# A two-layer transformer trunk on one core: elementwise sums and products of two SBUF tiles all on VectorE, and new prices in the order planner

## The chip, the cores and the metric

The kernel runs on one core of a Trainium2 chip. The metric is the device time of one execution in microseconds. Before the change the median of 3 runs is 1422.42 us (1422.35 to 1424.1).

In the profile the engines are PE (TensorE matmul), PEld (TensorE weight load), DVE (VectorE), ACT (ScalarE), POOL (GpSimd) and SP (SyncE, which issues the DMAs here).

## The reference

The reference is a trunk of two layers on 512 tokens of width 1024, all in float32. Each layer is three residual blocks with a norm before and after:

```
for layer in range(2):
    y = mixer(rms_norm(x, g[0]));            x = x + rms_norm(y, g[1])
    y = memory_cross_attention(rms_norm(x, g[2]), rms_norm(mem, mem_norm_g), ...)
    x = x + rms_norm(y, g[3])
    y = swiglu(rms_norm(x, g[4]), wg, wu, wd);   x = x + rms_norm(y, g[5])
```

The mixer of layer 0 joins 8 heads of forgetting attention (softmax with a cumulated log gate) with 8 heads of sparse attention (compressed, selected and window branches with gates, partial rotary embedding on q and k). The mixer of layer 1 is differential attention of 8 heads (two softmaxes, p = a1 - lam * a2) with a norm on each head. The cross attention has 4 heads over 256 memory tokens. The SwiGLU has width 2816: `(silu(h @ wg) * (h @ wu)) @ wd`.

## The kernel before

Every float32 operand of a large product is split in two float32r parts, hi and lo = x - hi, and a product is three matmuls: hi*hi, hi*lo, lo*hi (`mm`). So each tile of weights or activations needs one copy to hi (ScalarE) and one subtraction to lo (VectorE, `split`, line 556). Weights come in tiles of 128x1024 ("raw"), 3 buffers, and go to pairs of "w", "pt" or "u" tiles.

Tokens stand in four blocks of 128. The stages in order of time: norm and projections of layer 0, forgetting attention, sparse attention, then `last_heads` (line 965), in which each token block goes through `chain` (line 849): output projection, `post_norm` (line 643), cross attention, a second `post_norm`, and the norm before the SwiGLU. Then `ffn` (line 999) with 22 columns blocks of 128 in groups of three (`up` makes one), ending in `post_norm` again. Layer 1 repeats this with the differential attention. `post_norm` takes a row of 1024 in two halves. Where the product stands in PSUM, it multiplies it with the factor and the gain into a tile "q" and adds that to x; where it stands in SBUF, it multiplies by the gain and then adds. For the first half (i = 0) this sum or product of two SBUF tiles is on GpSimd, for the second on VectorE. The factor comes from `rstd` (line 611): squares with a row sum on ScalarE, a sum on VectorE, and a power on GpSimd (the rows `c<-c,mhalf`). In `up`, the lo part of the activation is a subtraction on GpSimd, 22 to a layer.

The order of the instructions on all queues isn't that of the source. `note` (line 135) records every operation with its dependences and a price in ns (`price`, line 182); `order` (line 215) plans up to 14 rounds forward (`forward`, line 284) and backward (`backward`, line 239) in a list schedule over the five engines, keeps the round with the shortest planned span, and `issue` (line 487) emits it; so all profile rows have line 491. TensorE operations also have a `load`: the planned least time from the start of the one before to its own. `lend` (line 398) lets GpSimd take a waiting VectorE sum, difference or product of SBUF tiles where VectorE's planned backlog is long enough; the emitted engine is then GpSimd. The planner knows nothing of an engine slowing another.

Of the kernel before, what the change touches and what calls it, by code (L numbers as in the profile page):

```python
# [11 lines left out]
F32 = mybir.dt.float32  # L12
F32R = mybir.dt.float32r
# [4 lines left out]
PSUM = bass.MemoryType.PSUM  # L18
# [7 lines left out]
DH = 64  # L26
# [7 lines left out]
LAM_INIT = 0.8 - 0.6 * math.exp(-0.3 * 1)  # L34
LEAD = 2
KA = 6
ROWS = slice(0, DH), slice(DH, P)
ORDER = 0, 4, 5, 6, 7, 1, 8, 9, 10, 11, 12, 13, 2, 3
FILL0, FILL1, STAGE, LATE = 0.0, 1.2, 2.0, 30
# [48 lines left out]
class Plan:  # L88
# [9 lines left out]
    NEAR, FEW = 10000.0, 12  # L98
    AHEAD, EARLY, RING = 50000.0, 60000.0, 8
    ALPHA, BETA = 1.0, 2.0  # L100
    FLEX, MORE, HOLD = 100.0, 1.5, 5000.0

    def __init__(self, nc):
        self.nc = nc
# [30 lines left out]
    def note(self, eng, method, args, kw):  # L135
        aps = [("out" if i == 0 else "in", v) for i, v in enumerate(args) if isinstance(v, bass.AP)]
        if "out" in kw or "out_" in kw:
            aps = [("in", v) for _, v in aps]
        aps += [("out" if k in ("out", "accum_out") else "in", v) for k, v in kw.items() if isinstance(v, bass.AP)]

        op = dict(eng=eng.name, call=(eng, method, args, kw), cost=0.0, deps=set(), tiles=set(), prio=len(self.ops))
        i = len(self.ops)
        for kind, ap in aps:
            if ap.space == bass.MemoryType.DRAM and not str(ap.tensor.name).startswith("xsave"):
                continue
            name, p0, p1, mask = self.region(ap)
            if name in self.tags:
                op["tiles"].add(name)
            acc = self.seen.setdefault(name, ([], []))
            for w in (0,) if kind == "in" else (0, 1):  # L150
                for j, q0, q1, m in acc[w]:
                    if q0 < p1 and p0 < q1 and m & mask:
                        op["deps"].add(j)
            if ap.space == PSUM and kind == "in":

                op["deps"].update(j for j, *_ in acc[1] if self.ops[j]["eng"] != eng.name)
            acc[0 if kind == "out" else 1].append((i, p0, p1, mask))
        op["deps"].discard(i)
        op["group"] = i
        op["dma"] = method == "dma_start"  # L160
        if method == "matmul" and not kw["start"]:
            op["group"] = self.last_group[args[0].tensor.name]
        if method == "matmul":
            self.last_group[args[0].tensor.name] = op["group"]
        op["cost"] = self.price(eng.name, method, args, kw, [v for _, v in aps])

        op["alt"] = {}
        if eng.name == "vector" and method in ("tensor_sub", "tensor_add", "tensor_mul") and op["cost"] > self.FLEX \
                and all(ap.space != PSUM for _, ap in aps):
            op["alt"]["gpsimd"] = self.price("gpsimd", method, args, kw, [v for _, v in aps])  # L170
        op["load"] = 53.0 if method != "matmul" else self.free(args[1]) / (1.2 if args[1].dtype == F32R else 2.4)
        self.ops.append(op)
        return op

# [7 lines left out]
    def price(self, eng, method, args, kw, aps):  # L182
        n = max([self.free(a) for a in aps] + [1])
        if method == "dma_start":
            size = 1
            for _, k in aps[0].ap:
                size *= k
            return size * 4 / 360.0
        if eng == "tensor":
            if method == "transpose":  # L190
                return 107.0
            c = self.free(args[2]) / 2.4
            return max(25.0, 2.5 + (c if args[2].dtype == F32R else 4 * c))
        if eng == "scalar":
            extra = sum(isinstance(kw.get(k), bass.AP) for k in ("bias", "scale", "accum_out"))
            return (52 if aps[1].space == PSUM else 95) + 0.83 * n + 93 * extra
        if eng == "vector":
            psum = any(a.space == bass.MemoryType.PSUM for a in aps)
            n = n + 62 * sum(isinstance(v, bass.AP) and self.free(v) == 1 for v in args[2:3])
            if method == "reciprocal":  # L200
                return 60 + 8 * n
            if method in ("tensor_copy", "tensor_scalar", "memset") and not psum:
                return 65 + 0.52 * n
            return 65 + 1.04 * n
        if eng == "gpsimd":
            if method == "tensor_tensor":
                return 260 + 200 * n
            if method in ("tensor_sub", "tensor_add", "tensor_mul"):
                return 100 + 2.3 * n
            if method == "memset":  # L210
                return 30 + 0.84 * n
            return (322 if len(aps) > 3 else 222) + 0.84 * n
        raise ValueError(method)

    def order(self):
        ops = self.ops
        n = len(ops)
        self.eng0 = [o["eng"] for o in ops]
        self.succ = [[] for _ in range(n)]
        for i, o in enumerate(ops):  # L220
            for j in o["deps"]:
                self.succ[j].append(i)
        best = None
        prio = [float(o["prio"]) for o in ops]
        for _ in range(self.ROUNDS):
            for i, o in enumerate(ops):
                prio[o["group"]] = min(prio[o["group"]], prio[i])
            prio = [prio[o["group"]] for o in ops]
            for k, o in enumerate(self.firsts):
                prio[o["group"]] = k - 1e9  # L230
            r = self.forward(prio, self.AHEAD - best[0] if best else math.inf)
            if best is None or r[0] < best[0]:
                best = r
            prio = self.backward(r)
        self.span, self.at, self.fin, out = best[:4]
        self.eng = best[5]
        return out

    def backward(self, run):

        span, at, fin, out, reuse, eng = run
        ops, n = self.ops, len(self.ops)
        pred = [list(o["deps"]) for o in ops]
        for j, i in reuse:
            pred[i].append(j)
# [5 lines left out]
        ready = {e: [] for e in engines}  # L251
# [6 lines left out]
        while ev:  # L258
            now = ev[0][0]
# [4 lines left out]
            for e in engines:  # L264
                h = ready[e]
                while h and busy[e] <= now + 1e-9:
                    i = heapq.heappop(h)[1]
                    cost = ops[i]["cost"] if eng[i] == self.eng0[i] else ops[i]["alt"][eng[i]]
                    end = now + cost
                    if ops[i]["dma"]:  # L270
                        end += 2000
# [11 lines left out]

    def forward(self, prio, far):

        ops, eng, succ = self.ops, list(self.eng0), self.succ
        n = len(ops)
        left = [len(o["deps"]) for o in ops]
        users, queue = {}, {}
# [105 lines left out]
                    heapq.heappush(heap, (top, i))  # L395
            return found

        def lend(e, f):

            wait = busy[e] - now  # L400
            for top, i in sorted(ready[e]):
                c = ops[i]["alt"].get(f)
                if c and wait > self.MORE * (c - ops[i]["cost"]) \
                        and not any(at[j] < now + c and prio[j] < top + self.HOLD for j in soon[f]):
                    ready[e].remove((top, i))
                    heapq.heapify(ready[e])
                    eng[i] = f
                    heapq.heappush(ready[f], (top, i))
                    return
                wait += ops[i]["cost"]  # L410

        while done < n:
            if not events:
                raise RuntimeError(f"no order found; stuck on {sorted(stuck)} at instruction {min(set(range(n)) - set(out))} of {n}")
# [18 lines left out]
            again = True  # L433
            while again:
                again = False
                if busy["gpsimd"] <= now + 1e-9 and not ready["gpsimd"] and busy["vector"] > now:
                    lend("vector", "gpsimd")
                for e, heap in ready.items():
                    while heap and busy[e] <= now + 1e-9:
                        if e in ("vector", "scalar", "gpsimd"):  # L440
# [8 lines left out]
                        o = ops[i]  # L449
                        out.append(i)  # L450
                        done += 1
                        cost = o["cost"] if e == self.eng0[i] else o["alt"][e]
                        if o["dma"]:
                            at[i] = now
                            busy[e] = now + 60
# [22 lines left out]
                        for j in succ[i]:  # L478
                            left[j] -= 1
                            at[j] = max(at[j], fin + self.LAT.get(e[0] + eng[j][0], 100.0))  # L480
                            if not left[j]:
                                heapq.heappush(events, (at[j], seq, "op", j))
                                soon[eng[j]].add(j)
                                seq += 1
        return max(ends), at, ends, out, reuse, eng

    def issue(self, tc):
        with tc.manual_schedule():
# [5 lines left out]
class Trunk:  # L494
# [148 lines left out]
    def post_norm(self, ys, g, x, tb):  # L643

        nc = self.nc
        r = self.rstd(ys)
        c0 = 0
        for i, y in enumerate(ys):
            s = slice(c0, c0 + y.shape[-1])
            c0 = s.stop  # L650
            if ys[i].space == PSUM:
                h = self.qtile()
                nc.vector.scalar_tensor_tensor(h, ys[i], r, g[:, s], op0=ALU.mult, op1=ALU.mult)
                (nc.vector if i else nc.gpsimd).tensor_add(x[tb][:, s], x[tb][:, s], h)
            else:
                (nc.vector if i else nc.gpsimd).tensor_mul(ys[i], ys[i], g[:, s])
                nc.vector.scalar_tensor_tensor(x[tb][:, s], ys[i], r, x[tb][:, s], op0=ALU.mult, op1=ALU.add)

    def xtile(self):
# [339 lines left out]
    def ffn(self, l, x, hT):  # L999
# [5 lines left out]
        def up(c):  # L1005
# [11 lines left out]
            nc.vector.scalar_tensor_tensor(b, th, 0.5, pu, op0=ALU.mult, op1=ALU.mult)  # L1017
            at = acts[c] = self.unit()
            nc.scalar.activation(at[:, 0:512], b, AF.Copy)
            nc.gpsimd.tensor_sub(at[:, 512:1024], b, at[:, 0:512].bitcast(F32))  # L1020

        where = self.pt_tiles
        yacc = None
# [622 lines left out]
```

## Time and profile before

| | us |
|---|---|
| median of 3 runs | 1422.42 |
| the profiled execution, its own time | 1422.67 |
| span of its trace, first to last instruction | 1421.0 |
| mean granted TensorE clock, share of full | 0.996 |

The span is what the rows below divide; 1.67 us of the profiled execution's own time lie outside it. Busy time of an engine is the time in which at least one of its instructions runs; matmuls are pipelined, so a busy TensorE may still be short of its peak rate. A row "x6" of a timeline is six like instructions in one stretch. Times in timelines are from the start of the span.

### The profile page before, as it was taken

The numbers are of one execution on the slowest core, as the hardware profiler recorded it, in microseconds if no ns is written. First come the engines' busy times: TensorE is split into PE (matmuls) and PEld (weight loads), VectorE is DVE, ScalarE is ACT, GpSimd is POOL, SyncE is SP. The second block draws the span as 40 slices with busy tenths as digits, with TensorE's granted clock in tenths as the row PEclk, the third lists the DMA queues.
The fourth block names the chain that finished last, engine by engine and source line by source line (L and its number), as shares of the span: only waits on it lengthen the run. The fifth ranks groups of instructions, "written<-read, shape, count | busy, mean of one in ns | idle before, by whom it ended". The sixth has DMA issues, their size and how long they took to land.

```text
span 1421.0 us, 21566 instructions
## 1 busy us (share of the span) xinstructions
PE 1383.2 (97%) x8003; PEld 1204.0 (85%) x8003; DVE 833.7 (59%) x1851; ACT 725.0 (51%) x1606; POOL 355.9 (25%) x429
## 2 busy tenths in 40 slices
PE   7999999999899999999999999999989999999997
PEld 6788988889788888888889999988878888888886
DVE  5667899498842333433466888876984233343344
ACT  5768879488643122223245677786863322222322
POOL 2203334244320121012031233312552012101202
PEclk9999999999999999999999999999999999999999
DMA  7251112321233233324321321243234323332411
GB/s 218 65 150 47 46 45 87 107 74 61 89 119 89 89 104 90 114 78 134 105 74 54 95 91 61 77 147 104 85 92 121 89 84 110 89 108 85 119 60 60
DMA packets 150425, 132.05 MB, mean 93 GB/s; under 512 B 6928, under 2 KB 134096, under 8 KB 150320
## 3 DMA queue, kind: packets, MB, share of 16 engines
q1 hardware_dynamic: 150320, 130.67, 30.2%
q8 instruction: 63, 1.03, 0.3%
q14 instruction: 42, 0.34, 0.1%
HBM read 126.26 MB, written 4.19 MB: 92 GB/s over the span
## 4 chain that ended last, share of the span: by engine, by line
PE 84%; DVE 7%; ACT 3%; DMA 2%; POOL 2%; issue 2%; SPq 0%; POOLq 0%; DVEq 0%; ACTq 0%
PE ps L491 84%; DVE q L491 2%; DVE x L491 1%; DVE u L491 1%; ACT q L491 1%; DVE c L491 1%; DMA raw<-in_ev_w_in_dram 1%; POOL c L491 1%; POOL q L491 1%; ACT u L491 1%; DVE pt L491 1%; DMA pt<-in_ev_w_in_dram 0%; DVE w L491 0%; ACT pt L491 0%; POOL x L491 0%
## 5 line engine op out<-in xcount | busy, mean ns | idle before, releaser
L491 PE MATMUL ps<-hThi,w 128*128 128x512 f32 (+1 forms) x1664 | 488.0, 375 | 2.6 <-DVE q L491 2.6
L491 PEld LDWEIGHTS ps<-hThi,w 128*128 128x128 f32 x1664 | 306.5, 190 | 58.3 <-ACT junk L491 1.6
L491 PE MATMUL ps<-hTlo,w 128*128 128x512 f32 (+1 forms) x832 | 311.6, 375 | 0.4 <-DVE hTlo L491 0.2
L491 PE MATMUL ps<-w,hThi 128*128 128x256 f32 (+2 forms) x1280 | 281.9, 316 | 2.3 <-ACT hThi L491 2.3
L491 DVE TENSOR_TENSOR w<-raw,w 128x1024 fp32r<-128x1024 f32 (+1 forms) x136 | 170.2, 1268 | 152.3 <-issue 72.8
L491 ACT ACTIVATE w<-raw 128x1024 fp32r<-128x1024 f32 (+1 forms) x153 | 158.4, 1051 | 164.4 <-PE ps L491 138.7
L491 PE MATMUL ps<-pt,u 128*128 128x512 f32 (+3 forms) x1126 | 231.8, 338 | 1.4 <-DVE pt L491 0.8
L491 PEld LDWEIGHTS ps<-w,hThi 128*128 128x128 f32 x1280 | 210.5, 192 | 15.2 <-ACT hThi L491 3.2
L491 DVE TENSOR_TENSOR u<-ps,u 128x512 f32<-128x512 f32 (+6 forms) x278 | 150.6, 546 | 116.4 <-PE ps L491 98.0
L491 PEld LDWEIGHTS ps<-pt,u 128*128 128x128 f32 (+1 forms) x1126 | 175.2, 173 | 31.6 <-DVE pt L491 1.5
L491 POOL TENSOR_TENSOR u<-q,u 128x512 fp32r<-128x512 f32 x44 | 64.0, 1454 | 542.7 <-ACT u L491 542.7
L491 PE MATMUL ps<-w,hTlo 128*128 128x256 f32 (+2 forms) x640 | 199.8, 313 | 0.0
L491 PE MATMUL ps<-u 128*128 128x512 f32 (+4 forms) x806 | 186.4, 348 | 0.1
L491 PEld LDWEIGHTS ps<-hTlo,w 128*128 128x128 f32 x832 | 158.0, 190 | 28.3 <-DVE hTlo L491 1.3
L491 PEld LDWEIGHTS ps<-u 128*128 128x128 f32 (+1 forms) x806 | 131.1, 183 | 18.4 <-DVE pt L491 0.4
L491 DVE SCALAR_TENSOR_TENSOR q<-q,ps 128x512 f32<-128x512 f32 x88 | 60.3, 686 | 141.1 <-PE ps L491 103.5
L491 ACT ACTIVATE u<-ps 64x256 fp32r<-64x256 f32 (+6 forms) x269 | 116.0, 438 | 51.8 <-PE ps L491 47.4
L491 ACT ACTIVATE q<-ps 128x256 f32<-128x256 f32 (+6 forms) x158 | 72.7, 460 | 119.0 <-PE ps L491 117.4
L491 PEld LDWEIGHTS ps<-w,hTlo 128*128 128x128 f32 x640 | 122.4, 192 | 7.2 <-DVE hTlo L491 0.8
L491 PE MATMUL ps<-ident,q 128*128 128x128 f32 (+1 forms) x645 | 109.6, 278 | 18.0 <-DVE q L491 13.8
L491 PEld LDWEIGHTS ps<-ident,q 128*128 128x128 f32 (+1 forms) x645 | 77.5, 141 | 28.3 <-DVE q L491 11.5
L491 ACT ACTIVATE q<-q,c 128x128 f32<-128x128 f32 (+3 forms) x160 | 88.7, 557 | 12.7 <-DVE c L491 11.8
(151 smaller groups left out, 1518.1 us busy)
## 6 DMA issues: line engine op xcount, KB each, us to landing
raw<-in_ffn_wg_dram SPq DMA_DIRECT2D x44, 512.0 KB
raw<-in_ffn_wu_dram SPq DMA_DIRECT2D x44, 512.0 KB
raw<-in_ffn_wd_dram SPq DMA_DIRECT2D x44, 512.0 KB
raw<-in_od_w_in_dram SPq DMA_DIRECT2D x24, 512.0 KB
raw<-in_ev_w_in_dram SPq DMA_DIRECT2D x16, 512.0 KB
u<-in_sandwich_g_dram SPq DMA_DIRECT2D x10, 512.0 KB
x<-in_x_dram SPq DMA_DIRECT2D x8, 512.0 KB
raw<-in_ev_w_out_dram SPq DMA_DIRECT2D x8, 512.0 KB
```

Source lines behind the costliest of these rows:

```text
L491: getattr(getattr(self.nc, self.eng[i]), method)(*args, **kw)
```

## The change

Three things change. In the source, `post_norm` and `up` use VectorE for what GpSimd did. `lend` goes, with the prices it used, so that nothing is moved from VectorE to GpSimd by the order either. And the prices change: a matmul of over 240 columns costs columns/2.4 + 13 ns (it was + 2.5), a shorter one + 6.5; a transpose 109 (was 107); ScalarE and VectorE operations whose first operand (the output) has 64 rows and that have over 100 elements a row cost 115 ns more; the `load` of a float32r matmul is stationary columns/2.4 (it was /1.2, that is 53 in place of 107 ns for 128). The order on every queue is computed anew from these prices.

```diff
-        op["alt"] = {}
-        if eng.name == "vector" and method in ("tensor_sub", "tensor_add", "tensor_mul") and op["cost"] > self.FLEX \
-                and all(ap.space != PSUM for _, ap in aps):
-            op["alt"]["gpsimd"] = self.price("gpsimd", method, args, kw, [v for _, v in aps])
-        op["load"] = 53.0 if method != "matmul" else self.free(args[1]) / (1.2 if args[1].dtype == F32R else 2.4)
+        op["load"] = 53.0 if method != "matmul" else self.free(args[1]) / 2.4
...
-                return 107.0
+                return 109.0
             c = self.free(args[2]) / 2.4
-            return max(25.0, 2.5 + (c if args[2].dtype == F32R else 4 * c))
+            return max(25.0, (13.0 if c > 100 else 6.5) + (c if args[2].dtype == F32R else 4 * c))
+        half = HALF_ROWS if eng in ("scalar", "vector") and n > 100 and aps[0].ap[0][1] == DH else 0
...
-            return (52 if aps[1].space == PSUM else 95) + 0.83 * n + 93 * extra
+            return (52 if aps[1].space == PSUM else 95) + 0.83 * n + 93 * extra + half
...
-            return 65 + 1.04 * n
+            return 65 + 1.04 * n + half
...
-                if busy["gpsimd"] <= now + 1e-9 and not ready["gpsimd"] and busy["vector"] > now:
-                    lend("vector", "gpsimd")
...
-                (nc.vector if i else nc.gpsimd).tensor_add(x[tb][:, s], x[tb][:, s], h)
+                nc.vector.tensor_add(x[tb][:, s], x[tb][:, s], h)
             else:
-                (nc.vector if i else nc.gpsimd).tensor_mul(ys[i], ys[i], g[:, s])
+                nc.vector.tensor_mul(ys[i], ys[i], g[:, s])
...
-            nc.gpsimd.tensor_sub(at[:, 512:1024], b, at[:, 0:512].bitcast(F32))
+            nc.vector.tensor_sub(at[:, 512:1024], b, at[:, 0:512].bitcast(F32))
```

`HALF_ROWS` is 115, `DH` is 64. The rest of the diff takes out `lend`, its constants and the second set of engines that `forward` and `backward` passed on for it.

## Rows read from the trace of the kernel before

**Rows 1.** Page, busy time: busy us (share of the span) xinstructions.
```profile
PE 1383.2 (97%) x8003; PEld 1204.0 (85%) x8003; DVE 833.7 (59%) x1851; ACT 725.0 (51%) x1606; POOL 355.9 (25%) x429
```

**Rows 2.** Windows: stretch, length, busy of PE, PEld, DVE, ACT, POOL, clock, DMA share, GB/s.
```profile
140.00:260.00 120.00, 117.72 (x866) 107.32 (x865) 102.35 (x371) 96.05 (x258) 47.60 (x68) 1.00 0.20 64
354.00:376.00 22.00, 16.68 (x115) 13.89 (x113) 20.34 (x32) 18.89 (x46) 12.70 (x13) 0.90 0.15 49
371.00:378.00 7.00, 5.54 (x26) 5.12 (x26) 6.56 (x10) 3.90 (x9) 2.57 (x3) 0.55 0.36 118
390.00:752.00 362.00, 362.00 (x1693) 303.28 (x1693) 149.26 (x184) 107.57 (x150) 64.03 (x42) 1.00 0.32 98
752.00:960.00 208.00, 205.59 (x1603) 197.56 (x1602) 164.56 (x500) 156.36 (x429) 58.42 (x99) 1.00 0.28 90
1032.00:1052.00 20.00, 15.00 (x108) 12.20 (x107) 17.68 (x28) 17.05 (x40) 15.33 (x14) 1.00 0.17 54
```

**Rows 3.** Groups of GpSimd by shape: busy us, mean ns, idle before.
```profile
L491 POOL TENSOR_TENSOR u<-q,u 128x512 fp32r<-128x512 f32 x44 | 64.0, 1454 | 542.7 <-ACT u L491 542.7
L491 POOL TENSOR_TENSOR w<-raw,w 128x1024 fp32r<-128x1024 f32 x17 | 51.3, 3015 | 30.7 <-issue 20.1 <-PE ps L491 10.6
```

**Rows 4.** Groups of VectorE by shape.
```profile
L491 DVE TENSOR_TENSOR w<-raw,w 128x1024 fp32r<-128x1024 f32 x133 | 167.4, 1276 | 150.5 <-issue 72.8 <-PE ps L491 56.3 <-ACT w L491 11.3
L491 DVE TENSOR_TENSOR u<-u 128x512 f32<-128x512 f32 x11 | 7.5, 680 | 0.0
```

**Rows 5.** Timeline of 1040 to 1043: start, length, engine and operation.
```profile
1040.34 1.25 POOL L491 TENSOR_TENSOR x<-x,q 128x512 f32<-128x512 f32 x1
1040.40 1.75 DVE L491 SCALAR_TENSOR_TENSOR q<-x,c,u 128x512 f32<-128x512 f32 x1 [0.27 <-POOL c L491]
...
1042.40 0.74 DVE L491 SCALAR_TENSOR_TENSOR q<-x,c,u 128x512 f32<-128x512 f32 x1
```

**Rows 6.** Chain that ended last, within 354 to 376: start, length, what.
```profile
366.74 2.92 POOL x L491 x2
...
370.41 1.47 POOL c L491
```

**Rows 7.** The same chain within 1016 to 1066.
```profile
1040.40 3.42 DVE q L491 x4
...
1043.89 1.29 POOL x L491
1045.17 0.51 POOL c L491
1045.68 1.24 POOL x L491
```

**Rows 8.** Timeline of 1411 to 1415, the last matmuls and their eviction.
```profile
1412.49 1.30 POOL L491 TENSOR_TENSOR u<-u 128x512 f32<-128x512 f32 x1 [1.55 <-ACT junk L491]
1412.68 1.66 DVE L491 SCALAR_TENSOR_TENSOR x<-u,c,x 128x512 f32<-128x512 f32 x1
...
1412.86 0.88 PE L491 MATMUL ps<-u 128*128 128x256 f32 x6
...
1414.33 0.41 DVE L491 TENSOR_TENSOR u<-ps,u 128x256 f32<-128x256 f32 x1
```

**Rows 9.** Groups of GpSimd in 140 to 260, those with two tiles.
```profile
L491 POOL TENSOR_TENSOR hTlo<-x,hThi 128x512 fp32r<-128x512 f32 x2 | 2.5, 1287 | 0.0
L491 POOL TENSOR_TENSOR w<-raw,w 128x1024 fp32r<-128x1024 f32 x1 | 2.4, 2406 | 0.0
```

**Rows 10.** Groups of GpSimd in 752 to 960, those with two tiles.
```profile
L491 POOL TENSOR_TENSOR w<-raw,w 128x1024 fp32r<-128x1024 f32 x2 | 5.3, 2659 | 0.7 <-PE ps L491 0.7
L491 POOL TENSOR_TENSOR q<-rope 128x64 f32<-128x64 f32 x12 | 4.0, 330 | 17.3 <-DVE rope L491 16.6 <-ACT q L491 0.6
```

**Rows 11.** Timeline of ScalarE, 776 to 786: a run of 64-row copies.
```profile
776.23 3.90 ACT L491 ACTIVATE u<-ps 64x256 fp32r<-64x256 f32 x10
```

**Rows 12.** Timeline of TensorE, 104 to 108: a run of short matmuls.
```profile
104.61 2.71 PE L491 MATMUL ps<-u 128*128 128x128 f32 x16
```

More of the change, by code (lines that the diff above doesn't have):

```diff
@@ L36 @@
 KA = 6
+HALF_ROWS = 115
 ROWS = slice(0, DH), slice(DH, P)
@@ L100 @@
     ALPHA, BETA = 1.0, 2.0
-    FLEX, MORE, HOLD = 100.0, 1.5, 5000.0
     def __init__(self, nc):
@@ L207, in price @@
                 return 260 + 200 * n
-            if method in ("tensor_sub", "tensor_add", "tensor_mul"):
-                return 100 + 2.3 * n
             if method == "memset":
@@ L217, in order @@
         n = len(ops)
-        self.eng0 = [o["eng"] for o in ops]
+        self.eng = [o["eng"] for o in ops]
         self.succ = [[] for _ in range(n)]
@@ L235, in order @@
         self.span, self.at, self.fin, out = best[:4]
-        self.eng = best[5]
         return out
     def backward(self, run):
-        span, at, fin, out, reuse, eng = run
-        ops, n = self.ops, len(self.ops)
+        span, at, fin, out, reuse = run
+        ops, eng, n = self.ops, self.eng, len(self.ops)
         pred = [list(o["deps"]) for o in ops]
@@ L267, in backward @@
                     i = heapq.heappop(h)[1]
-                    cost = ops[i]["cost"] if eng[i] == self.eng0[i] else ops[i]["alt"][eng[i]]
+                    cost = ops[i]["cost"]
                     end = now + cost
@@ L284, in forward @@
     def forward(self, prio, far):
-        ops, eng, succ = self.ops, list(self.eng0), self.succ
+        ops, eng, succ = self.ops, self.eng, self.succ
         n = len(ops)
@@ L396, in pick @@
             return found
[L398 to L410, printed above, removed]
         while done < n:
@@ L451, in forward @@
                         done += 1
-                        cost = o["cost"] if e == self.eng0[i] else o["alt"][e]
+                        cost = o["cost"]
                         if o["dma"]:
@@ L484, in forward @@
                                 seq += 1
-        return max(ends), at, ends, out, reuse, eng
+        return max(ends), at, ends, out, reuse
     def issue(self, tc):
```

## The prediction

> **What bounds the kernel now.** I read the page's busy times first. TensorE is busy 1383.2 of 1421.0 us [rows 1]; no other engine comes near, so nothing on VectorE or GpSimd counts for itself, only where TensorE waits for it. At most 37.8 us (1421.0 - 1383.2) of visible waiting can be won, all reasons together.
>
> Then the windows, to see where those waits lie. In the SwiGLU of layer 0 (390 to 752) TensorE is busy 362.00 of 362 us, VectorE 149.26 [rows 2]; layer 1's runs the same code. There an edit on VectorE or GpSimd is free as long as the lo parts come in time. The waits stand in the attention stretches and most thickly at their two ends, where the last token blocks run through the norms alone: 5.32 us idle in the 22 us from 354 (22.00 - 16.68) and 5.00 in the 20 us from 1032 (20.00 - 15.00) [rows 2]. The crowded stretches before them lose less: 2.28 us in 140 to 260, 2.41 in 752 to 960, though VectorE is busy 102.35 of 120 and 164.56 of 208 there [rows 2].
>
> Last the chain that ended last, in those two ends. It runs through GpSimd: two adds of x halves, 2.92 us, then a power of a 128x1 column that takes 1.47 [rows 6]; in the second end, four VectorE products, 3.42 us, then adds on GpSimd of 1.29 and 1.24 with a power of 0.51 between [rows 7]. These adds are the ones that the change moves.
>
> **The moved work, and its price.** GpSimd gives up 44 subtractions of the SwiGLU (64.0 us, 1454 ns each) and 17 weight splits that the order had lent it (51.3 us, 3015 ns each) [rows 3], with the eight products and eight sums of the norms and some small pieces. VectorE does a 128x512 form of two SBUF tiles in 680 ns and a split in 1276 [rows 4]: 44 x 0.68 + 17 x 1.276 = 29.9 + 21.7 = 51.6 us, and 16 x 0.68 = 10.9 for the norms. VectorE goes from 833.7 to about 896, 63% of the span.
>
> The trace also shows a second price. The same VectorE product `q<-x,c,u` takes 1.75 us when it starts beside a GpSimd add of 1.25 us, and 0.74 alone two us later [rows 5]; 1040.40 + 1.75 ends 0.56 after GpSimd's 1041.59, so most of its work came when GpSimd was through. GpSimd's split of 3015 ns is 2406 in a less busy place [rows 3, 9]. So the two engines wait for each other when both read two SBUF tiles, and the move takes away these waits with the slow operation. The Trainium skill, "SBUF — State Buffer", section "SBUF: two separate sides", says that the port pair is an exclusive lock and that a GpSimd operation and a VectorE operation with two SBUF inputs block each other for the whole instruction; by it the powers and scalings that stay on GpSimd would now be blocked by more VectorE operations. By rows a power takes 0.51 free and 1.47 at worst [rows 6, 7], 0.96 more; that is in the bounds below.
>
> **Step by step**, against the profiled execution's own 1422.67 us (1421.0 span, 1.67 around it; the median of the runs is 1422.42, 0.25 lower):
>
> SwiGLU: 22 subtractions a layer and at most seven splits (17 less the three of rows 9 and 10, over two layers), 22 x 0.68 + 7 x 1.276 = 23.9 us more on a VectorE that has 362 - 149.26 = 212.7 us to spare. Nothing, -0.0. TensorE's own queue covers it; if that cover went, each late lo part would cost less than before, since 0.68 replaces 1.454.
>
> First end (354 to 376): two adds 2 x 0.68 = 1.36 in place of 2.92, -1.56 at best; with the power no longer blocked -2.5. But VectorE is busy 20.34 of 22 [rows 2], so the adds stand in a queue. At worst they gain nothing, and 0.96 is lost on another blocked power. I take -1.0.
>
> Second end (1032 to 1052): the product falls from 1.75 to 0.74, the add beside it joins VectorE's queue with 0.68: -0.33. The adds of 1.29 and 1.24 become 0.68 each: -1.17. Sum -1.5, bounds -2.5 (the first add slips out of the chain, power and queue permitting) and +0.96 (as above).
>
> Tail: VectorE's last big product takes 1.66 in place of 0.74 beside a GpSimd product of 1.30; the last matmuls end at 1412.86 + 0.88 = 1413.74, but their eviction starts only at 1414.33 [rows 8]. With the GpSimd product on VectorE, 1412.68 + 0.74 + 0.68 = 1414.10, or the eviction goes first. Between 0 and -0.59; I take -0.3.
>
> Crowded stretches: in 140 to 260 one split and two lo parts of 512 move, 1.276 + 2 x 0.68 = 2.64 us more VectorE work; in 752 to 960 two splits and twelve rotary sums, 2 x 1.276 + at most 4.0 = 6.55 [rows 4, 9, 10]. Both stretches have VectorE idle time (17.65 and 43.44 us), and TensorE shows 4.69 idle in both. At worst all 9.2 us become late; at best the waits go, -4.7.
>
> Prices: they reorder every queue, so they decide here. In the trace six matmuls of 256 columns take 0.88 us [rows 8]; that is five starts of the new 119.7 ns (106.7 + 13) and 0.28 for the last to run through, where the old 109.2 would need 0.33. Ten ScalarE copies of 64x256 take 3.90 us, 0.39 each [rows 11]; the old price was 52 + 0.83 x 256 = 264, the new 379. So the new plan's clock runs closer to the chip's on TensorE and on the 64-row copies. One price gets worse: 16 matmuls of 128 columns take 2.71 us [rows 12], 0.17 each; the plan now lets them follow at 60 ns, before at 107. A plan that is right about when TensorE needs its operands should wait less; how much no row shows. I take -2.0 for the two crowded stretches together, somewhat under half of their 4.69, with +9.2 and -4.7 as ends.
>
> Sum: 0 - 1.0 - 1.5 - 0.3 - 2.0 = -4.8, so 1422.67 - 4.8 = 1417.9.
>
> **The rivals.**
>
> The wait only changes its name. At both ends VectorE is the busiest engine but TensorE (20.34 of 22, 17.68 of 20); what GpSimd no longer delays then waits in VectorE's queue. For it: the first end leaves VectorE 1.66 us free, and two moved adds take 1.36 of it. Against it: part of that busy time is blocked time, 1.01 in rows 5 alone. Ends and crowded stretches give nothing, the tail stays: 1422.67 - 0.3 = 1422.4.
>
> VectorE becomes the bound in the crowded stretches: slower. In 140 to 260 it is busy 85%, and lending took its overflow. The place is the split of attention weights and the rotary sums ahead of the transposes; it decides once VectorE's queue has no gap ahead of what TensorE takes next. The 2.64 us in full, half of the 6.55, and no gain at the ends: +5.9 - 0.3, so 1428.3; the near half of the case lies at 1425 to 1427. Against it: TensorE loses only 4.69 us in both stretches now. The Trainium skill, "Perfetto Trace Analysis", section "Optimizing Scalar/DVE Operations", speaks for this rival: a saturated VectorE may be relieved by moving work to other engines, even GpSimd; the same passage warns that these two share a port and that it might not help. Rows 5 show the warning at work, so it raises this rival's chance little.
>
> The better plan fills far more. The granted clock in 371 to 378 is 0.55 [rows 2], so some 6.3 of 7 us ran at 1.2 GHz in place of 2.4, after TensorE had idled at the end of layer 0's attention; that costs 3.15 us. The same idling in 1032 to 1052 shows 1.00, so it needn't happen. If it goes and another 5 of the 37.8 us fill up: 1417.9 - 3.15 - 5 = 1409.8. Against it: nothing in the change aims at that place but two adds; and a new fall in the second end would cost as much the other way.
>
> **Numbers.** Forecast 0.48, its own range 1413 to 1421. The wait that changes its name 0.22; VectorE as the bound 0.17; the much better plan 0.13. A measurement of this kernel tells about 0.2%, 2.8 us, from no change. Faster (under 1419.6): 0.13, and 0.46 of the forecast's 0.48, 0.59. Within: the 0.22 and the forecast's rest, 0.24. Slower (over 1425.3): 0.17. The range goes from 1407, under the better plan, to 1427, through the near half of the slower case; about a tenth is left out on each side.
>
> **What would show it.** The group rows of GpSimd have no two-tile form but the power; VectorE's `q<-x,c,u` and `x<-u,c,x` stay near 0.74 us each time; the longest splits end near 1.23; VectorE's busy time is about 896. The two ends show under 5.3 and 5.0 us of idle TensorE, with VectorE adds of 0.68 in the chain where `POOL x` stood. SwiGLU stretches keep their length to a us. The prediction is wrong if TensorE's idle time grows in 140 to 260 or 752 to 960 with waits for VectorE, if the ends keep their idle time under another name, or if the clock falls at a new place.

## The result, and the profile after

The changed kernel takes 1412.45 us (median of 4 runs, 1412.01 to 1413.14); the kernel before took 1423.26 in the same comparison. The ratio is 0.9925, with a 95% interval of 0.9907 to 0.9942: faster, by 0.6 to 0.9%. The profiled executions are 1422.67 and 1412.43 us, 10.2 us apart; 4.8 were forecast. The time lies in the range of 1407 to 1427, but a little under the forecast's own range of 1413 to 1421.

The page after, busy time, answers to [rows 1]:

```profile
PE 1380.1 (98%) x8003; PEld 1203.7 (85%) x8003; DVE 881.9 (63%) x1973; ACT 726.4 (51%) x1606; POOL 191.6 (14%) x307
```

VectorE has taken on 48.2 us and GpSimd given up 164.3: VectorE ends at 881.9 where some 896 were forecast, since it no longer stands still beside GpSimd. The groups of VectorE after (busy us, mean ns) show it, beside [rows 4, 5] and one more row of before, which comes last: a split takes 1228 ns in the mean and no longer 1276, the product `q<-x,c,u` 748, which is its time alone, and no longer 918.

```profile
L468 DVE TENSOR_TENSOR w<-raw,w 128x1024 fp32r<-128x1024 f32 x150 | 183.2, 1228 | 106.6 <-PE ps L468 94.1 <-ACT w L468 11.8
L468 DVE TENSOR_TENSOR u<-q,u 128x512 fp32r<-128x512 f32 x44 | 30.2, 687 | 10.5 <-ACT u L468 10.5
...
L468 DVE SCALAR_TENSOR_TENSOR q<-x,c,u 128x512 f32<-128x512 f32 x32 | 22.8, 748 | 3.3 <-POOL c L468 3.2
```
```profile
L491 DVE SCALAR_TENSOR_TENSOR q<-x,c,u 128x512 f32<-128x512 f32 x32 | 28.5, 918 | 4.2 <-POOL c L491 4.0
```

The windows after, columns as in [rows 2]:

```profile
140.00:260.00 120.00, 118.16 (x873) 108.54 (x872) 103.94 (x375) 97.16 (x259) 37.45 (x61) 1.00 0.18 58
354.00:376.00 22.00, 18.30 (x121) 16.09 (x120) 20.71 (x36) 15.66 (x38) 6.59 (x7) 0.92 0.26 79
366.00:371.00 5.00, 4.64 (x26) 4.52 (x27) 5.00 (x9) 3.33 (x7) 0.55 (x1) 0.66 0.01 3
390.00:752.00 362.00, 362.00 (x1695) 303.50 (x1694) 172.77 (x227) 109.35 (x160) 9.61 (x12) 1.00 0.32 98
752.00:960.00 208.00, 205.78 (x1576) 197.56 (x1575) 163.11 (x512) 155.82 (x422) 49.42 (x79) 1.00 0.31 96
1032.00:1052.00 20.00, 18.14 (x149) 16.72 (x147) 18.55 (x33) 13.76 (x31) 3.83 (x6) 1.00 0.24 73
```

The SwiGLU is as it was, TensorE busy 362.00 of 362, with 23.5 us more on VectorE. The ends lose less: 3.70 and 1.86 us of idle TensorE where [rows 2] give 5.32 and 5.00; the second window isn't quite the same work, since the whole stands 8 us earlier. In 366 to 371 the granted clock is 0.66, so about 3.4 of 5 us ran at 1.2 GHz and not at 2.4. Before, the fall took 6.8 us, a little more than the window of [rows 2] holds. Half of the difference, 1.7 us, is about what the first end gains in the table below.

Windows of fixed times mislead once the kernels run apart. So I cut each trace by the number of the TensorE instruction that starts (8003 in each). The lengths of the pieces in us, from the instructions' start times (the last one up to the end of VectorE's last operation):

| TensorE instructions | before | after | e1 | e3 | e8 | e4 |
|---|---|---|---|---|---|---|
| to 125, start | 32.1 | 30.8 | 32.0 | 30.8 | 30.7 | 30.8 |
| 125 to 1000, projections, first attention | 143.1 | 142.4 | 142.4 | 144.2 | 143.0 | 143.7 |
| 1000 to 2000, attention of layer 0 | 149.4 | 146.1 | 150.1 | 155.8 | 147.0 | 146.6 |
| 2000 to 2400, first end | 59.0 | 57.4 | 58.2 | 57.9 | 55.0 | 55.5 |
| 2400 to 3900, SwiGLU | 325.5 | 325.5 | 325.5 | 325.5 | 325.4 | 325.4 |
| 3900 to 6000, its end, attention of layer 1 | 298.0 | 296.9 | 297.3 | 297.6 | 297.6 | 296.9 |
| 6000 to 7990, second end, SwiGLU | 405.0 | 403.2 | 408.1 | 407.6 | 404.0 | 401.3 |
| rest, the tail | 5.88 | 5.35 | 5.58 | 5.88 | 5.89 | 5.34 |

From before to after, by the unrounded lengths: the ends give 1.6 and 1.8, the tail 0.5, and the other pieces 6.3, of it 3.2 in the attention of layer 0.

The chain that ended last, within 340 to 390 after, beside [rows 6]:

```profile
354.15 0.60 DVE x L468
...
357.74 1.54 POOL c L468
359.29 0.02 issue
359.31 0.92 DVE q L468 x2
...
361.26 1.47 POOL c L468
```

VectorE's add of 0.60 stands where GpSimd's took half of 2.92. But the power still takes 1.54 and 1.47: it waits for VectorE's two-tile operations, as before, the first time for two adds `x<-x,q`, the second for a split.

The tail after, beside [rows 8]:

```profile
1402.99 0.74 DVE L468 SCALAR_TENSOR_TENSOR x<-u,c,x 128x512 f32<-128x512 f32 x1
...
1403.16 0.88 PE L468 MATMUL ps<-u 128*128 128x256 f32 x6
...
1404.08 0.42 DVE L468 TENSOR_TENSOR u<-ps,u 128x256 f32<-128x256 f32 x1 [0.21 <-PE ps L468]
1404.42 0.68 DVE L468 TENSOR_TENSOR u<-u 128x512 f32<-128x512 f32 x1
```

The big product takes 0.74 for 1.66, and the eviction starts 0.04 us after the last matmul's end at 1404.04, where 0.59 passed before. The product that GpSimd had, the last row, now follows it.

### The profile page after: what moved, and what is told of

It is laid out like the page before. It is cut to its first block, busy times and chain, and to the rows that moved or that the text cites. A ratio compares the mean times of both kernels' runs of the same rounds, so it can differ in the third digit from the quotient of the medians.

```text
span 1410.7 us, 21537 instructions
## 1 busy us (share of the span) xinstructions
PE 1380.1 (98%) x8003; PEld 1203.7 (85%) x8003; DVE 881.9 (63%) x1973; ACT 726.4 (51%) x1606; POOL 191.6 (14%) x307
## 4 chain that ended last, share of the span: by engine, by line
PE 87%; DVE 7%; ACT 3%; issue 1%; POOL 1%; DMA 1%; SPq 0%; POOLq 0%; DVEq 0%; ACTq 0%
PE ps L468 87%; DVE q L468 2%; DVE u L468 1%; DVE x L468 1%; DVE c L468 1%; ACT junk L468 1%; POOL c L468 1%; DVE pt L468 1%; DVE w L468 1%; ACT q L468 1%; ACT u L468 1%; DVE hTlo L468 1%; DMA raw<-in_ev_w_in_dram 0%; POOL q L468 0%; DMA pt<-in_ev_w_in_dram 0%
## 5 line engine op out<-in xcount | busy, mean ns | idle before, releaser
L468 DVE TENSOR_TENSOR w<-raw,w 128x1024 fp32r<-128x1024 f32 (+1 forms) x153 | 186.0, 1223 | 108.3 <-PE ps L468 94.1
L468 ACT ACTIVATE u<-ps 64x256 fp32r<-64x256 f32 (+5 forms) x269 | 115.9, 438 | 61.9 <-PE ps L468 59.1
L468 POOL TENSOR_TENSOR c<-c,mhalf 128x1 f32<-128x1 f32 (+1 forms) x68 | 52.7, 777 | 560.5 <-DVE c L468 557.2
L468 PE MATMUL ps<-ident,q 128*128 128x128 f32 (+1 forms) x645 | 103.3, 277 | 15.3 <-DVE q L468 11.6
L468 ACT ACTIVATE pt<-raw 128x1024 fp32r<-128x1024 f32 x28 | 29.7, 1060 | 166.4 <-PE ps L468 107.0
L468 PEld LDWEIGHTS ps<-ident,q 128*128 128x128 f32 (+1 forms) x645 | 75.6, 141 | 25.2 <-DVE q L468 10.1
```

Of the source, the lines that this page charges most:

```text
L468: getattr(getattr(self.nc, self.eng[i]), method)(*args, **kw)
```

## The experiments

Ratios are against the kernel before in the same comparison, with the 95% interval. "Plan" is the order that the planner makes.

**e1: the old order, its operations on VectorE.** The kernel before; at emission alone:

```diff
-                getattr(getattr(self.nc, self.eng[i]), method)(*args, **kw)
+                e = "vector" if method in ("tensor_sub", "tensor_add", "tensor_mul") else self.eng[i]
+                getattr(getattr(self.nc, e), method)(*args, **kw)
```

> The kernel before, with its order kept instruction by instruction (planned with the lending and the old prices), but every sum, difference and product of two tiles that stood on GpSimd is emitted on VectorE at the same place of the order. Theory A (GpSimd's slow two-tile operations and the blocking between the two engines cost the time): most of the 10.2 us is won, -6 to -9 us. Theory B (the new prices gave the gain by a better order): -1 to -3 us, since the ends keep their order. Rival C (VectorE is the bound where it is crowded): +2 to +6 us.

Measured: 1.0017 (1.0008 to 1.0026), slightly slower. Theory A, by which this edit wins 6 to 9 us, falls: VectorE runs free, its splits take 1226 ns and `q<-x,c,u` 747, as the groups of this run show,

```profile
L492 DVE TENSOR_TENSOR w<-raw,w 128x1024 fp32r<-128x1024 f32 x150 | 180.9, 1226 | 142.0 <-PE ps L492 121.6 <-ACT w L492 9.6 <-ACT q L492 9.2
...
L492 DVE SCALAR_TENSOR_TENSOR q<-x,c,u 128x512 f32<-128x512 f32 x32 | 23.1, 747 | 2.6 <-POOL c L492 2.4
```

and nothing is won. The windows of the same run show that the clock falls in both ends (0.66 of 5 us and 0.51 of 7, some 5 us lost together where the kernel before lost 3.4), in the second for the first time. But the clock isn't the reason: of the runs with the same mean granted clock, 0.995, those of e1 take 1423.55 to 1425.18 us and those of the kernel before 1422.82 to 1423.86.

```profile
372.00:377.00 5.00, 3.99 (x19) 3.82 (x20) 5.00 (x7) 2.79 (x7) 0.00 (x0) 0.66 0.33 108
...
1049.00:1056.00 7.00, 6.34 (x28) 6.05 (x29) 6.56 (x12) 2.39 (x5) 1.04 (x2) 0.51 0.64 198
```

**e2: the new order, the source's operations on GpSimd.** The changed kernel; the first-half sums and products of `post_norm` and the subtractions of `up` are planned for VectorE and emitted on GpSimd:

```diff
-            nc.vector.tensor_sub(at[:, 512:1024], b, at[:, 0:512].bitcast(F32))
+            nc.vector.tensor_sub(at[:, 512:1024], b, at[:, 0:512].bitcast(F32))["emit"] = "gpsimd"
...
-                getattr(getattr(self.nc, self.eng[i]), method)(*args, **kw)
+                getattr(getattr(self.nc, self.ops[i].get("emit", self.eng[i])), method)(*args, **kw)
```

> The changed kernel, its order kept, but the 16 first-half sums and products of post_norm in the trunk's attention ends and SwiGLU ends and the 44 subtractions of the SwiGLU are emitted on GpSimd as before. Theory A: it loses 3 to 6 us against the changed kernel (the ends), and nothing in the SwiGLU. Theory B: it loses under 2 us.

Measured: 0.9957 (0.9944 to 0.9969), 1416.38 us; the change has 0.9925. So with the order kept, these operations are worth about 0.3%, some 4 us, but a change without them would still keep more than half of its gain. By the pieces of the table none of it is lost at the first end, 57.3 us against 57.4; 2.5 us are in 3900 to 6000, 1.0 in 6000 to 7990 and 0.5 in the tail. The groups show the blocking back: `q<-x,c,u` at 810 ns in the mean, GpSimd's add at 1576.

```profile
L468 DVE SCALAR_TENSOR_TENSOR q<-x,c,u 128x512 f32<-128x512 f32 x32 | 24.8, 810 | 2.9 <-POOL c L468 2.8
```
```profile
L468 POOL TENSOR_TENSOR x<-x,q 128x512 f32<-128x512 f32 x8 | 12.6, 1576 | 9.8 <-DVE q L468 9.8
```

**e3: the prices alone.** The kernel before with the price lines of the change's diff (load, transpose, matmul, `half`), nothing else.

> The kernel before with the new prices alone (matmul, transpose, load, 64 rows); lending and the source's GpSimd operations stay. Theory A: -1 to -3 us against before. Theory B: -6 to -9 us.

Measured: 1.0030 (1.0020 to 1.0041), 1426.91 us: slower, against both theories. Its windows show a fall of the clock in the midst of layer 0's attention, 0.61 over 13 us, and two more:

```profile
173.00:186.00 13.00, 13.00 (x75) 13.00 (x75) 7.06 (x28) 4.67 (x15) 0.32 (x1) 0.61 0.00 1
200.00:210.00 10.00, 9.56 (x73) 8.94 (x72) 9.83 (x46) 8.10 (x24) 4.01 (x8) 0.83 0.01 2
378.00:383.00 5.00, 4.76 (x26) 4.58 (x27) 4.55 (x8) 1.93 (x5) 2.69 (x2) 0.66 0.65 195
```

That is 10.1, 3.4 and 3.4 us at 1.2 GHz, some 8.4 lost (TensorE isn't idle in the first, 13.00 of 13, it is slow). This profiled execution was 1430.0, the slowest of its eight. The falls aren't all of the loss: with a mean clock of 0.997 it takes 1425.50, the kernel before 1421.10 to 1421.94.

**e4: the moves alone.** The changed kernel with the old prices:

```diff
-HALF_ROWS = 115
+HALF_ROWS = 0
...
-        op["load"] = 53.0 if method != "matmul" else self.free(args[1]) / 2.4
+        op["load"] = 53.0 if method != "matmul" else self.free(args[1]) / (1.2 if args[1].dtype == F32R else 2.4)
...
-                return 109.0
+                return 107.0
-            return max(25.0, (13.0 if c > 100 else 6.5) + (c if args[2].dtype == F32R else 4 * c))
+            return max(25.0, 2.5 + (c if args[2].dtype == F32R else 4 * c))
```

> The changed kernel with the old prices: all two-tile operations on VectorE, planned anew. Theory A: -7 to -9 us against before. Theory B: 0 to -4 us. If neither e3 nor e4 gains half of it, the two parts need each other.

Measured: 0.9913 (0.9900 to 0.9927), 1409.93 us. All of the gain is in the moves, planned anew; the lowest time of all here, though its interval overlaps the change's. Its windows at the first end show the clock at 1.00 and 2.84 us of idle TensorE:

```profile
354.00:376.00 22.00, 19.16 (x136) 16.40 (x135) 20.90 (x38) 16.67 (x42) 6.08 (x7) 1.00 0.23 67
```

After these four the theory was D: a plan that puts two-tile work on GpSimd can't be kept on the chip. Its rival was E: orders scatter, and the change drew a good one.

**e5 and e6: another round of the same planner.** The kernel before and that of e4, each with the order of a later round:

```diff
-        self.span, self.at, self.fin, out = best[:4]
+        self.span, self.at, self.fin, out = taken[:4]
...
```

`taken` is the ninth round in e5, the seventh in e6.

> The kernel before, but the order of the planner's ninth round is emitted (planned span 1319.43 us) in place of the best, the third (1318.49). Theory D (a plan with GpSimd's two-tile work can't be kept on the chip, a plan without it can): within 3 us of the kernel before, 1419 to 1425. Theory E (orders of almost the same planned span scatter by as much as the whole gain, and the change drew a good one): 5 us or more away on either side, 1411 to 1417 or above 1427.

> The kernel with the moves and the old prices (the one of 1409.93 us), but with the order of the planner's seventh round (planned span 1319.18 us in place of 1319.10). Theory D: 1407 to 1413. Theory E: 5 us or more away from 1409.9.

Measured: e5 0.9996 (0.9987 to 1.0005), e6 0.9924 (0.9912 to 0.9937). Each lies within 0.15% of its sister. So E falls as a cause of the whole, as far as one other round of each shows. e5 also shows that the 1.2 us of the start are no work of the change: its first 125 matmuls take 30.8 us, on the old rules.

**e7: the source's operations alone**, the last three replaced lines of the change's diff, on the kernel before. **e8: no lending alone**:

```diff
-                if busy["gpsimd"] <= now + 1e-9 and not ready["gpsimd"] and busy["vector"] > now:
-                    lend("vector", "gpsimd")
```

> The kernel before, where only the source's GpSimd operations (16 sums and products in the trunk's norms, 8 in the SwiGLU's, 44 subtractions) go to VectorE; lending and old prices stay, order planned anew. Theory D: about half of the gain, -3 to -7 us, since lending still puts splits on GpSimd near the ends. Theory E: anything between -10 and +5.

> The kernel before, where only the lending goes; the source's GpSimd operations and the old prices stay, order planned anew. Theory D: -2 to -6 us, the rest of the gain. Theory E: anything between -10 and +5, and e7 and e8 don't add up to the -12 of both.

Measured: e7 0.9987 (0.9978 to 0.9996), e8 0.9941 (0.9927 to 0.9955). The lending is the larger part, about 0.6% of the 0.9 of e4; and with lending left on, the source's moves hardly count: the planner lends 12 of the 44 subtractions back, and 16 splits. The page of e7 has GpSimd at 289.3 us, against 191.6 after:

```profile
PE 1382.5 (97%) x8003; PEld 1201.9 (85%) x8003; DVE 859.5 (61%) x1897; ACT 726.3 (51%) x1606; POOL 289.3 (20%) x383
```

In e8 GpSimd keeps the source's sums and subtractions, 64.8 us for the 44, and the first end still goes well, TensorE idle for 1.75 us and the clock at 1.00:

```profile
354.00:376.00 22.00, 20.25 (x147) 17.55 (x146) 20.75 (x35) 16.62 (x41) 11.29 (x11) 1.00 0.18 56
```

**e9 and e10: a planner that knows of the blocking.** To the kernel before (e9) and to e4 (e10), in `forward`; `pair` marks GpSimd's operations but memsets, and VectorE's with two SBUF tiles or from SBUF to SBUF:

```diff
                                 at[i] = now
+                                if o["pair"]:
+                                    at[i] = max(now, hold["vector" if e == "gpsimd" else "gpsimd"])
                             busy[e] = fin = at[i] + cost
+                            if o["pair"]:
+                                hold[e] = fin
```

> The kernel before, with one thing added to its planner: a VectorE operation with two SBUF tiles (or a copy or scalar operation between SBUF tiles) and any GpSimd operation but a memset can't start while one of the other kind runs. Lending, the source's GpSimd operations and the old prices stay. Theory D (the plan of before can't be kept because the engines block each other): -4 to -8 us. Theory F (lending is a poor choice of the planner in itself, whatever it knows of the blocking): within 2 us of the kernel before.

> The kernel with the moves and the old prices (1409.93 us), its planner knowing of the blocking as in e9; what stays on GpSimd are powers and scalings. Theory D: 1 to 4 us faster, 1406 to 1409. Theory F: 1409 to 1411.

Measured: e9 0.9989 (0.9977 to 1.0001), about 0.1% and no more, as theory F had it; e10 0.9948 (0.9937 to 0.9960), slower than e4, against both. So to tell the plan of the blocking doesn't mend the time. But e9's time hides two effects. Its runs spread from 1417.85 to 1425.65 us, in step with the granted clock: three at 0.988 take 1425.42 to 1425.65, two at 0.995 take 1417.85 and 1418.01, where the seven runs of the kernel before at 0.995 take 1422.06 to 1424.55 in the same comparison. The mean clock is 0.9915 in e9 and 0.9952 in the kernel before. At the same clock the order that knows of the blocking is 4 to 7 us faster, and it loses them to more falls of the clock. So e9 doesn't bear theory D out by its time, and doesn't refute it either; why its clock falls more often isn't shown.

**e12 and e13: the load price.** The changed kernel with the old `load` line (e12), and that with the blocking in the plan (e13).

> The changed kernel with one price taken back: the load of 128 float32r columns is 107 ns again in the plan, not 53. If that price is what made e3 slower: 1408 to 1411. If it is another one: 1412 to 1414.

> e12 with the planner knowing of the blocking as in e9. Theory D: 1 to 4 us faster than e12. Theory F: within 1 us of e12.

Measured: e12 0.9942 (0.9930 to 0.9955), e13 0.9934 (0.9922 to 0.9946). Neither shows that the load price is what made e3 slower; which of the prices did stays open. Nor does the blocking rule show a gain there: the intervals overlap, and e13 is within 1 us of e12, as theory F had it.

## Why the prediction was right, and where not

**All runs in one view.** The plans with lending have 1 (before), 1.0030, 0.9996, 0.9987 and 0.9989 (e3, e5, e7, e9), and e1, a lending order, 1.0017. Those without have 0.9925 (the change), 0.9957, 0.9913, 0.9924, 0.9941, 0.9948, 0.9942 and 0.9934 (e2, e4, e6, e8, e10, e12, e13). The two groups don't meet, whatever the prices and the rounds; within one, plans differ by 0.4%. So it is shown that taking the lending out makes most of the gain, with some 0.3% from the source's moves behind it, and that the new prices give none: e4 without them is as fast. It isn't shown by which mechanism.

**SwiGLU, nothing: right.** 325.5 and 325.5 us; VectorE's 149.26 [rows 2] became 172.77, 23.5 more where 23.9 were worked out.

**First end, -1.0, and second, -1.5: near in size, the first by luck.** They gave 1.6 and 1.8. For the first the prediction had adds leave the chain, and the runs show otherwise: e2 has them back on GpSimd, in the change's order, and this piece is as long, 57.3 us against 57.4; in e8, where they never left, it is 55.0. Its length goes with the clock. In the fourteen profiled executions it is 54.5 to 55.8 us in the six without a fall, 57.3 to 58.9 in the five with 3.4 us at 1.2 GHz, 58.8 and 59.0 with 6.8, and 61.7 with 10.2; the change has 3.4 where the kernel before had 6.8. The clock was put with the better plan, not here. The second end stays open: e2 gives back 1.0 of its 1.8, and e8 wins 1.1 without the moves. VectorE's queue stayed full in the first, 20.71 of 22 us.

The sentence of the Trainium skill, "SBUF — State Buffer", section "SBUF: two separate sides", on the blocking of whole instructions agrees with this trace on GpSimd's side: powers of 1.47 and 1.54 beside VectorE's two-tile operations. On VectorE's side it agrees in part: the product takes 748 ns in the mean once GpSimd has no two-tile work, but a product that starts 0.06 us into a power of 0.54, as after the change at 376.03, takes 0.75 all the same.

**Tail, -0.3: right.** It gave 0.5, near the bound of 0.59, for the eviction now goes ahead of the moved product. e2, with that product back on GpSimd, has the old tail of 5.89.

**Crowded stretches and prices, -2.0: the step that failed**, in size and in reason. The prediction said of the prices that "they decide here", and took the lending only as work for VectorE, 2.64 and 6.55 us. Measured is -6.3 (start 1.2, 0.7, 3.2 in layer 0's attention, 1.1 in layer 1's). 1.2 of it belong to the third round's start of the kernel before, as e5 shows; prices alone cost 0.3% (e3), and taking the lending out alone gives 0.6% (e8). Its counts were short as well, which doesn't change the sum much: the first-half sums and products of the norms are 24 and not 16 (e8's GpSimd has 12 `u<-u`, 8 `x<-x,q` and 4 `x<-x,u`), [rows 9, 10] leave out GpSimd's 128x64 `rope` forms, some 0.9 and 1.4 us of VectorE work, and the terms named for the second end's bound add up to -2.2 and not -2.5.

What the lent operations do on the path can be read in the trace. The timeline of the kernel before at 347.9, just ahead of the first end's window:

```profile
347.52 1.22 DVE L491 TENSOR_TENSOR w<-raw,w 128x1024 fp32r<-128x1024 f32 x1 [0.43 <-ACT w L491]
...
347.93 1.40 POOL L491 TENSOR_TENSOR q<-q 128x256 fp32r<-128x256 f32 x1 [1.21 <-issue]
...
349.38 0.96 PE L491 MATMUL ps<-w,q 128*128 128x512 f32 x3 [0.59 <-POOL q L491]
```

A lent lo part of 256 columns takes 1.40 us and TensorE waits 0.59 for it. After the change the same operation takes 0.41 on VectorE:

```profile
349.46 0.41 DVE L468 TENSOR_TENSOR q<-q 128x256 fp32r<-128x256 f32 x1
```

That is one of the places, but such waits are not what the change won: in all, TensorE waits for GpSimd 3.1 us before and 3.2 after. What fell is its idle time as a whole, from 37.8 us (1421.0 - 1383.2) to 30.6 (1410.7 - 1380.1), 7.2 of the 10.3 us by which the span is shorter, and most of that in waits for VectorE's `q`. Rows of TensorE's waits, columns: us in total, times, longest; before, then after:

```profile
PE ps L491 <- DVE q L491: 16.4, 9, 7.5
PE ps L491 <- POOL q L491: 2.5, 5, 0.9
...
PE ps L491 <- POOL x L491: 0.6, 2, 0.4
```
```profile
PE ps L468 <- DVE q L468: 11.6, 4, 7.5
PE ps L468 <- POOL q L468: 2.9, 5, 1.2
...
PE ps L468 <- POOL x L468: 0.3, 1, 0.3
```

So what the change won lies mostly in how long TensorE waits for VectorE, though VectorE has more work. Lent operations may stand one step behind those waits; that wasn't followed.

**What the clock has of it.** In the profiled executions, up to the tail, the plans with lending spent 6.8, 17.1, 13.7, 3.4 and 17.1 us at 1.2 GHz (before, e3, e5, e7, e9), 11.6 in the mean and so 5.8 lost at most; those without, in the same order as above, 3.4, 6.8, 0, 0, 0, 3.4, 0 and 6.8, a mean of 2.6, 1.3 lost. The mean granted clocks of all runs, tail included, say much the same (the span times what the clock lacks to 1.00): some 7.5 us lost in the plans with lending, 3.3 in those without. About 4 us, some half of what divides the groups, can be the clock. For the change itself it is less: 0.9970 in its four runs and 0.9952 to 0.9958 in those of the kernel before make about 2 of 10 us.

These are upper estimates, since a fall need not cost half its length. e2 and the change have the same TensorE order; e2 (first two rows) has a fall at 199.0 that the change (third row) doesn't have:

```profile
180.00:199.00 19.00, 18.70 (x166) 18.25 (x164) 17.99 (x91) 14.36 (x49) 7.15 (x12) 1.00 0.18 56
199.00:202.40 3.40, 3.04 (x15) 2.92 (x16) 3.40 (x16) 3.25 (x11) 1.21 (x2) 0.50 0.02 7
```
```profile
199.00:202.40 3.40, 2.53 (x17) 1.91 (x17) 3.40 (x16) 3.22 (x11) 1.21 (x2) 1.00 0.01 2
```

TensorE waits less in e2's stretch in place of ending later: its instruction 1300, at 211.2 us, starts within 0.01 us of the change's.

**Why lending makes a worse order stays open.** To take the blocking away under the finished order wins nothing (e1). To tell the planner of it wins 4 to 7 us at the same clock and nothing in the median (e9). The price of lent work is no rival apart from that: the plan has 100 + 2.3 x 256 = 689 ns for the operation above, and GpSimd's two forms of 256 columns that ran beside no two-tile work of VectorE take 738 in the mean; the 1400 above ran beside the split that starts at 347.52. What that price leaves out is the blocking. A planner that knows of the blocking and of the clock wasn't tried.

**The rivals.** "The wait only changes its name" is what e1 does, the same edit without a new plan. "VectorE becomes the bound" didn't come: 140 to 260 has VectorE busy 103.94 of 120 and TensorE idle 1.84, where 2.28 were [rows 2]. The passage of the Trainium skill, "Perfetto Trace Analysis", section "Optimizing Scalar/DVE Operations", speaks for moving work off a saturated VectorE; here such lending cost 0.6% (e8), with VectorE busy 85% in 140 to 260. The warning of the same passage, that it might not help, fits e8, though no run shows that the shared port is the whole reason. "The better plan fills far more", 1409.8, came nearest in time, but not by better prices.

## What to carry to other kernels

Before pricing moved work by its busy time, follow a few of the moved operations in the timeline to who waits for them: a slow engine that takes work "for free" can stand on the path, here for 0.59 us at one place. To know whether a list-scheduled kernel gained by an edit or by its new order, emit the old order with the edit and the new order without it, and another round of each plan as a measure of scatter. A planner's prices that fit the chip better need not give a better order. And compare orders at the same granted clock as well as by their medians: e9's median hid an order that was 4 to 7 us better at the same clock.

## What the runs showed of the hardware

GpSimd's one-tile work slows VectorE little in sum: after the change 132 of the 150 splits meet no GpSimd operation and take 1222 ns in the mean, the other 18 take 1276. VectorE's two-tile work slows GpSimd's powers much: a 128x1 power takes 0.51 free in the chain [rows 7], 1.47 beside a split and 1.54 beside two adds.

The clock can fall without a long idle stretch ahead: in the 19 us before e2's fall at 199.0 TensorE is busy 18.70 us, and its longest gap is 0.21. And the same TensorE order can meet a fall in one run and not in the other: the changed kernel has the same gap there, and no fall.
